# The second half of a layer's triangular solves moves from VectorE to GpSimd

## The chip, the cores and the metric

The kernel runs on one core of a Trainium2 chip. Its time is the device time of one execution in microseconds. A profiled execution also leaves a trace: when each instruction ran on TensorE (PE, with its weight loads PEld), VectorE (DVE), ScalarE (ACT) and GpSimd (POOL), and when SyncE (SP) issued DMAs.

## The reference

A two-layer network on 1040 tokens (16 learned ones ahead of 1024), width 1024. Layer 0 mixes with an attention and a state-space part, layer 1 with a gated delta rule of eight heads of width 128; an MLP follows each. Only layer 1's mixer matters here. With chunks of the sequence it computes, for each head, keys, queries and values (a product with a weight, a convolution over four tokens, silu), and then

```
lower = where(strict, beta * (k k^T) * decay, 0)
sol   = triangular_solve(I + lower, [v*beta, k*beta*exp(gcum)])
...                     # a scan over the chunks carries a 128x128 state
o     = rms_norm(o) * silu(z);  out = o @ w_out
```

## The kernel before

Products in float32 accuracy are made of three TensorE passes: weights and activations are split in a high part and a remainder, and high x high, high x low and low x high are summed in PSUM (L176, L177, L178). A weight tile comes by a DMA into one of two `wraw` buffers (L156), VectorE casts the high part (L165), and GpSimd subtracts for the remainder `wlo` (L166); four buffers of each hold weights ahead of their use.

Layer 1's mixer first makes the keys of the eight heads, then the queries, then per head the values and a gate. `conv_in` multiplies one tile of 128 features in three pieces of up to 352 tokens, each in one of three PSUM banks, and VectorE copies each piece out (L1343, tile `cx`). `conv_silu` scales on ScalarE (L1353), adds three shifted copies on VectorE (L1359, three instructions of 1040 elements) and applies silu on ScalarE (L1360, tile `cy`). `queries` then transposes on TensorE (L1469), reduces squares (L1471, L1472, norms `rq`), multiplies keys and queries (L1482, taken out by L1484), and multiplies by the decays on GpSimd in place (L1490).

The inverse of a 128 x 128 unit triangular matrix per head and chunk is made of blocks: four diagonal blocks of 32 x 32 are inverted alone, and `combine` joins them by products on TensorE (L1562 to L1587). The diagonal blocks of four heads, eight chunks and four blocks are 128, one for each partition. `solve_heads(half)` loads them (L1512, tile `sN`), `solve` inverts them (tile `sU`), and the result is stored (L1516), copied transposed on GpSimd (L1518) and stored again (L1520). Half 0 is heads 0 to 3, half 1 heads 4 to 7. `solve` takes 31 steps, each a product and a sum of an outer product's size:

```
v.tensor_tensor(p3, U3[:, 0:j, m]..., N3[:, m, m + 1:]..., op=ALU.mult)   # L1504
v.tensor_add(U3[:, 0:j, m + 1:], U3[:, 0:j, m + 1:], p3)                  # L1505
```

with j = m+1 and 31-m columns, so (m+1)(31-m) elements a partition: 31 in the first step, 256 in the middle, 31 in the last. Every instruction needs the one before it. A third, small solve (`solve_first`, tiles `U0` and `N0`, 16 x 16 on eight partitions) does the same for the sixteen leading tokens. Which engine runs a solve is a bit of the constant `SVE`:

```
yield from self.solve(128, 32, N, U, nc.gpsimd if SVE >> half & 1 else v)        # L1514
yield from self.solve(8, 16, N0, U0, nc.gpsimd if SVE >> 2 & 1 else nc.vector)   # L1530
```

The code writes instructions in one sequence, in which strands (keys and queries of even and odd heads, solves, combines, later chains, values and gates) take turns between the products. A scheduler of the framework then sorts them into one fixed order for each engine; semaphores make an engine wait where it needs another's result, and then all that stands behind waits too. The solve of half 1 can start when the keys of head 7 are done.

Of the kernel before, what the change touches and what calls it, by code (L numbers as in the profile page):

```python
# [1938 lines left out]
J3 = 2.5  # L1939
J4 = 5.0  # L1940
J5 = 4.0
CT, SVE, CJ = 0, 0, 0


PERIOD = 2
# [44 lines left out]
CT = 0  # L1990
# [53 lines left out]
CT = 0  # L2044
# [110 lines left out]
```

## Time and profile before

| | us |
|---|---|
| median of 3 runs (2943.26 to 2947.31) | 2943.39 |
| profiled execution | 2941.94 |
| its span, first to last instruction | 2940.1 |
| TensorE busy (94% of the span) | 2767.3 |
| VectorE busy (59%) | 1745.5 |
| GpSimd busy (44%) | 1307.8 |
| ScalarE busy (36%) | 1063.0 |

The second solve stands on VectorE from about 1703 to 1780 us of the span. The times below count from the span's start. In a timeline row stand the start, the duration, engine, line, operation, output and inputs, shapes and, in brackets, how long the engine was idle before it and what ended that. A group row has count, busy us and mean ns. A waits row has total us, times and the longest.

### The profile page before, as it was taken

What the parts mean: (1) busy time and instruction counts of PE and PEld (TensorE: products, weight loads), DVE (VectorE), ACT (ScalarE), POOL (GpSimd) and SP (SyncE); (2) the same over time, 40 slices, a digit from 0 to 9 for tenths busy, and PEclk for the clock granted to TensorE, in tenths of its full rate; (3) what the DMA queues carried; (4) which work ended last, traced back from release to release, by engine and by line L of the source; (5) the groups of instructions that cost most, each with busy time, mean ns of one, the idle gap of its engine ahead of it and who ended that gap; (6) DMA issues with size and microseconds to landing.
All of it is one profiled execution on the core that took longest, in us unless ns stands there. A gap on an engine that the chain in (4) does not pass through costs nothing. (4 is left out here: it accounts for less than half of the span.)

```text
span 2940.1 us, 44176 instructions
## 1 busy us (share of the span) xinstructions
PE 2767.3 (94%) x16488; PEld 2504.2 (85%) x16488; DVE 1745.5 (59%) x3107; ACT 1063.0 (36%) x2112; POOL 1307.8 (44%) x946
## 2 busy tenths in 40 slices
PE   7899999899999999999897978999998999999998
PEld 7689667788999999999887977899898888888887
DVE  8642768666755565555746896545538544444445
ACT  4111656554533332111436422433435433331101
POOL 5552325325577766432632123111125777664423
PEclk9889667889999999999998988999999999999999
DMA  3435312124333344221437667444334333442222
GB/s 129 158 121 157 80 57 80 49 87 166 129 116 115 100 142 152 90 85 44 140 88 221 195 201 235 127 132 149 109 117 153 107 109 111 136 165 93 95 82 89
DMA packets 209766, 360.99 MB, mean 123 GB/s; under 512 B 45488, under 2 KB 131200, under 8 KB 209552
## 3 DMA queue, kind: packets, MB, share of 16 engines
q1 hardware_dynamic: 205664, 353.49, 37.3%
q10 hardware_dynamic: 3888, 4.69, 0.4%
q8 instruction: 130, 2.13, 0.3%
q14 instruction: 84, 0.69, 0.1%
HBM read 247.07 MB, written 111.03 MB: 122 GB/s over the span
## 5 line engine op out<-in xcount | busy, mean ns | idle before, releaser
L166 POOL TENSOR_TENSOR wlo<-wraw,whi 128x1024 fp32r<-128x1024 f32 x125 | 305.0, 2452 | 730.5 <-ACT whi L163 238.7
L176 PE MATMUL mm<-ahi,whi 128*128 128x344 f32 (+2 forms) x1200 | 416.5, 348 | 41.3 <-DVE cx L1343 28.1
L178 PE MATMUL mm<-ahi,wlo 128*128 128x344 f32 (+2 forms) x1200 | 398.6, 332 | 2.3 <-DVE wlo L166 2.3
L177 PE MATMUL mm<-hl,whi 128*128 128x352 f32 (+4 forms) x1136 | 386.5, 340 | 0.0
L564 DVE TENSOR_TENSOR acc<-mm,acc 128x344 f32<-128x344 f32 (+4 forms) x308 | 177.3, 576 | 173.0 <-PE mm L178 173.0
L176 PEld LDWEIGHTS mm<-ahi,whi 128*128 128x128 f32 x1200 | 234.2, 195 | 50.2 <-DVE cx L1343 29.8
L178 PE MATMUL mm<-hh,wlo 128*128 128x352 f32 (+4 forms) x752 | 259.0, 344 | 2.5 <-POOL wlo L547 2.5
L176 PE MATMUL mm<-hh,whi 128*128 128x352 f32 (+4 forms) x752 | 259.2, 345 | 0.6 <-DVE acc L564 0.6
L178 PEld LDWEIGHTS mm<-ahi,wlo 128*128 128x128 f32 x1200 | 233.9, 195 | 4.3 <-DVE wlo L166 3.2
L564 DVE TENSOR_TENSOR acc<-tr,acc 128x344 f32<-128x344 f32 (+2 forms) x260 | 152.9, 588 | 139.7 <-PE tr L178 139.7
L177 PEld LDWEIGHTS mm<-hl,whi 128*128 128x128 f32 x1136 | 216.7, 191 | 11.1 <-issue 0.4
L178 PE MATMUL tr<-hh,wlo 128*128 128x512 f32 (+2 forms) x560 | 196.1, 350 | 0.0
L177 PE MATMUL tr<-hl,whi 128*128 128x512 f32 (+2 forms) x560 | 195.9, 350 | 0.0
L176 PE MATMUL tr<-hh,whi 128*128 128x512 f32 (+2 forms) x560 | 195.8, 350 | 0.0
L163 ACT CAST whi<-wraw 128x1024 fp32r<-128x1024 f32 x73 | 73.6, 1045 | 311.6 <-PE tr L177 287.2
L229 POOL TENSOR_TENSOR hl<-hr,hh 128x1040 fp32r<-128x1040 f32 (+1 forms) x56 | 135.6, 2431 | 76.4 <-ACT hh L228 53.7
L178 PEld LDWEIGHTS mm<-hh,wlo 128*128 128x128 f32 x752 | 142.1, 189 | 13.5 <-POOL wlo L547 3.1
L176 PEld LDWEIGHTS mm<-hh,whi 128*128 128x128 f32 x752 | 142.2, 189 | 10.9 <-DVE acc L564 0.9
L440 POOL TENSOR_TENSOR wlo<-sS,whi 128x512 fp32r<-128x512 f32 x104 | 144.4, 1391 | 13.6 <-ACT whi L439 13.4
L244 POOL TENSOR_TENSOR ssq<-ssq,sq 128x344 f32<-128x344 f32 (+2 forms) x84 | 90.9, 1082 | 84.5 <-ACT sq L243 76.4
L177 PE MATMUL mm<-hh,whi 128*128 128x344 f32 (+2 forms) x384 | 128.2, 334 | 0.0
L366 POOL TENSOR_TENSOR ssq_o<-ssq_o,sq 128x344 f32<-128x344 f32 (+4 forms) x84 | 93.9, 1118 | 76.4 <-ACT sq L365 75.9
(530 smaller groups left out, 7808.4 us busy)
## 6 DMA issues: line engine op xcount, KB each, us to landing
wraw<-w SPq DMA_DIRECT2D x128, 512.0 KB, 3.6
wraw<-wino SPq DMA_DIRECT2D x32, 512.0 KB, 5.2
hr<-hd SPq DMA_DIRECT2D x28, 520.0 KB, 5.5
hr<-hd SPq DMA_DIRECT2D x28, 512.0 KB, 4.3
dm<-dmd SPq DMA_DIRECT2D x16, 520.0 KB, 4.8
hsd<-hs SPq DMA_DIRECT2D x48, 172.0 KB, 1.9
hd<-u SPq DMA_DIRECT2D x52, 130.0 KB, 2.0
hd<-u SPq DMA_DIRECT2D x26, 256.0 KB, 2.8
```

What stands on the lines that cost most here:

```text
L163: nc.scalar.copy(hi[:, :n], raw[:, :n])
L166: (nc.vector if fast else nc.gpsimd).tensor_sub(lo[:, :n], raw[:, :n], f(hi[:, :n]))
L176: nc.tensor.matmul(pt, wh, h[:, o:o + n], start=i == 0, stop=False)
L177: nc.tensor.matmul(pt, wh, l[:, o:o + n], start=False, stop=False)
L178: nc.tensor.matmul(pt, wl, h[:, o:o + n], start=False, stop=i == len(kts) - 1)
L229: (lo_eng or nc.vector).tensor_sub(lo, src, f(hi))
L244: nc.gpsimd.tensor_add(st["ssq"][:, o:o + n], st["ssq"][:, o:o + n], sq[:, :n])
L366: nc.gpsimd.tensor_add(ssq[:, o:o + n], ssq[:, o:o + n], sq[:, :n])
L440: nc.gpsimd.tensor_sub(lo, src, f(hi))
L564: nc.vector.tensor_add(acc[m][:, o:o + n], pt, acc[m][:, o:o + n])
```

## The change

One constant: bit 1 of `SVE` is set, so that the solve of half 1 is issued to GpSimd. Its two memsets, 31 products and 31 sums move; the solve of half 0 and the small one stay on VectorE. No later line sets `SVE` again.

```diff
-CT, SVE, CJ = 0, 0, 0
+CT, SVE, CJ = 0, 2, 0
```

The scheduler sorts anew, so other instructions move too. Three places follow; numbers in names tell buffers apart.

VectorE, around the copy-out of the product of query head 5 (`cx_17147`; `mm_17149`, `mm_17179` and `mm_17212` are its three PSUM pieces), before:

```order
L1504 TENSOR_TENSOR sprod_17087<-sU_17079,sN_17078 128x220
L1505 TENSOR_TENSOR sU_17079<-sU_17079,sprod_17087 128x10x22
L1504 TENSOR_TENSOR sprod_17087<-sU_17079,sN_17078 128x231
L1343 TENSOR_TENSOR cx_17147<-mm_17149,rb_14159 128x352
L1343 TENSOR_TENSOR cx_17147<-mm_17179,rb_14159 128x344
L1343 TENSOR_TENSOR cx_17147<-mm_17212,rb_14159 128x344
L1359 SCALAR_TENSOR_TENSOR cy_17135<-cx_16543,gains_64,cy_17135 128x1040
L1505 TENSOR_TENSOR sU_17079<-sU_17079,sprod_17087 128x11x21
```

and after the change (`cy_17135` is query head 2, `U0` the small solve):

```order
L1359 SCALAR_TENSOR_TENSOR cy_17135<-cx_16543,gains_64,cy_17135 128x1040
L1504 TENSOR_TENSOR sprod_16937<-U0_16903,N0_16902 8x39
L1359 SCALAR_TENSOR_TENSOR cy_17135<-cx_16543,gains_64,cy_17135 128x1040
L1505 TENSOR_TENSOR U0_16903<-U0_16903,sprod_16937 8x13x3
L1359 SCALAR_TENSOR_TENSOR cy_17135<-cx_16543,gains_64,cy_17135 128x1040
L1504 TENSOR_TENSOR sprod_16937<-U0_16903,N0_16902 8x28
L1343 TENSOR_TENSOR cx_17147<-mm_17149,rb_14159 128x352
L1505 TENSOR_TENSOR U0_16903<-U0_16903,sprod_16937 8x14x2
L1343 TENSOR_TENSOR cx_17147<-mm_17179,rb_14159 128x344
```

The steps of half 1 are gone from VectorE; the copy-out now stands behind the three additions of head 2 and ahead of the end of the small solve.

GpSimd, behind the remainder `wlo_17264` of the weight for query head 7, before:

```order
L166 TENSOR_TENSOR wlo_17264<-wraw_17261,whi_17263 128x1024
L1490 TENSOR_TENSOR cy_16876<-cy_16876,eg_17083 128x1024
L1518 COPY sN_16186<-sU_16187 128x32x32
L166 TENSOR_TENSOR wlo_17440<-wraw_17437,whi_17439 128x1024
L166 TENSOR_TENSOR wlo_17739<-wraw_17736,whi_17738 128x1024
L1490 TENSOR_TENSOR cy_17034<-cy_17034,eg_17126 128x1024
```

After the change the solve's memsets and ten operations stand between the first and the second of these rows; in the middle of the solve stands:

```order
L1504 TENSOR_TENSOR sprod_17087<-sU_17079,sN_17078 128x252
L1505 TENSOR_TENSOR sU_17079<-sU_17079,sprod_17087 128x14x18
L1490 TENSOR_TENSOR cy_17034<-cy_17034,eg_17126 128x1024
L1518 COPY sN_16186<-sU_16187 128x32x32
L1339 MEMSET cx_17147 128x8
L1504 TENSOR_TENSOR sprod_17087<-sU_17079,sN_17078 128x255
```

Half 0's transposing copy (L1518) and query head 0's L1490 (`cy_17034`) now have 28 of the 62 operations ahead of them.

GpSimd, at the solve's end after the change:

```order
L1505 TENSOR_TENSOR sU_17079<-sU_17079,sprod_17087 128x27x5
L1504 TENSOR_TENSOR sprod_17087<-sU_17079,sN_17078 128x112
L1505 TENSOR_TENSOR sU_17079<-sU_17079,sprod_17087 128x28x4
L1504 TENSOR_TENSOR sprod_17087<-sU_17079,sN_17078 128x87
L166 TENSOR_TENSOR wlo_17440<-wraw_17437,whi_17439 128x1024
L1505 TENSOR_TENSOR sU_17079<-sU_17079,sprod_17087 128x29x3
```

The remainder `wlo_17440` of the weight for value head 0 stood ahead of query head 0's L1490 and now stands behind 57 operations of the solve; the next one, `wlo_17739`, comes later still.

## The prediction

> **What bounds the kernel now.** I read first the page's busy times, then the table by stretches around the solves, then TensorE's waits there, then the timelines of VectorE and GpSimd side by side.
>
> ```profile
> PE 2767.3 (94%) x16488; PEld 2504.2 (85%) x16488; DVE 1745.5 (59%) x3107; ACT 1063.0 (36%) x2112; POOL 1307.8 (44%) x946
> 1630.00:1686.00 56.00, 55.12 (x370) 52.97 (x369) 55.27 (x142) 22.75 (x48) 8.37 (x7) 1.00 0.56 182
> 1686.00:1724.00 38.00, 20.12 (x127) 19.48 (x127) 37.32 (x95) 5.68 (x7) 17.19 (x10) 0.77 0.56 198
> 1724.00:1741.00 17.00, 17.00 (x112) 16.84 (x113) 15.97 (x30) 4.43 (x6) 0.00 (x0) 0.91 0.61 187
> 1741.00:1784.00 43.00, 37.02 (x256) 35.83 (x255) 42.26 (x73) 11.35 (x14) 16.15 (x9) 0.93 0.71 246
> 1784.00:1816.00 32.00, 24.64 (x183) 22.65 (x182) 25.23 (x39) 7.83 (x11) 12.91 (x6) 0.93 0.61 193
> ```
>
> The first row is the whole span: TensorE is the bound. The others give, per stretch, its length and the busy time of PE, PEld, DVE, ACT and POOL, then the granted clock. From 1686 to 1784 us VectorE is busy 95.6 of 98 us and TensorE idles 23.9 us. Only what TensorE idles there can be won.
>
> ```profile
> 1699.05 1.12 PE L1469 MATMUL tr<-cst,cy 128*128 128x128 f32 x4 [4.83 <-ACT cy L1360]
> 1723.77 0.66 PE L176 MATMUL mm<-ahi,whi 128*128 128x352 f32 x1 [13.05 <-DVE cx L1343]
> 1763.86 0.63 PE L1469 MATMUL tr<-cst,cy 128*128 128x128 f32 x4 [2.13 <-DVE rq L1474]
> 1781.33 0.50 PE L176 MATMUL mm<-ahi,whi 128*128 128x352 f32 x1 [3.85 <-DVE cx L1343]
> ```
>
> Four stalls, 23.9 us, all behind VectorE (the first through ScalarE's silu, which waits for the last L1359). The largest is a product that wants a PSUM bank whose copy-out, L1343 of query head 5, stands on VectorE behind 21 operations of the second solve.
>
> **What leaves VectorE.** The second solve is two memsets and 62 products and sums.
>
> ```profile
> L1504 DVE TENSOR_TENSOR sprod<-sU,sN x31: 200/398/2342, 1704.5 to 1778.1; 128x31 f32<-128x31 f32 x2, 128x60 f32<-128x60 f32 x2, 128x87 f32<-128x87 f32 x2, 128x112 f32<-128x112 f32 x2
> L1505 DVE TENSOR_TENSOR sU<-sU,sprod x31: 172/373/2479, 1707.0 to 1779.4; 128x31 f32<-128x31 f32 x2, 128x60 f32<-128x60 f32 x2, 128x87 f32<-128x87 f32 x2, 128x112 f32<-128x112 f32 x2
> 1704.40:1780.00 75.60, 35.65 (x63) 2.36 (x2) 0.89 0.66 221
> 1703.25:1723.20 19.95, 15.15 (x24) 2.05 (x1) 0.75 0.60 214
> ```
>
> At the medians (398 and 373 ns) they would take 31 x 0.771 = 23.9 us; they took 35.65 us (third row, the operations on sU alone). The rest is waiting, and the next rows show for what. The last row says that 15.1 us of it, memset included, stand between 1703 us and the L1343 that TensorE waits for.
>
> **What that waiting is.** Rows of VectorE and GpSimd in the same microseconds:
>
> ```profile
> 1711.37 5.39 POOL L166 TENSOR_TENSOR wlo<-wraw,whi 128x1024 fp32r<-128x1024 f32 x2 [4.87 <-DVE whi L165]
> 1716.73 2.39 POOL L1490 TENSOR_TENSOR cy<-cy,eg 128x1024 f32<-128x1024 f32 x1
> 1712.24 2.32 DVE L1504 TENSOR_TENSOR sprod<-sU,sN 128x135 f32<-128x135 f32 x1
> 1714.60 2.32 DVE L1505 TENSOR_TENSOR sU<-sU,sprod 128x135 f32<-128x135 f32 x1
> 1716.95 2.34 DVE L1504 TENSOR_TENSOR sprod<-sU,sN 128x156 f32<-128x156 f32 x1
> 1719.33 0.32 DVE L1505 TENSOR_TENSOR sU<-sU,sprod 128x156 f32<-128x156 f32 x1
> 1723.20 1.36 DVE L1343 TENSOR_TENSOR cx<-mm,rb 128x352 f32<-128x352 f32 x3
> 1806.34 7.92 DVE L1359 SCALAR_TENSOR_TENSOR cy<-cx,gains,cy 128x1040 f32<-128x1040 f32 x3 [4.39 <-ACT cy L1353]
> 1806.56 6.59 POOL L1490 TENSOR_TENSOR cy<-cy,eg 128x1024 f32<-128x1024 f32 x2 [11.53 <-DMA eg<-gexp]
> 1649.88 1.12 DVE L1445 SCALAR_TENSOR_TENSOR nm<-tr,nb,dm 128x128 f32<-128x128 f32 x4
> 1650.10 2.39 POOL L166 TENSOR_TENSOR wlo<-wraw,whi 128x1024 fp32r<-128x1024 f32 x1 [12.90 <-PE tr L1442]
> ```
>
> A 0.3 us step with both inputs in SBUF lasts 2.32 us when GpSimd runs a 2.4 us subtraction, three times running: one of GpSimd, one of VectorE, one of GpSimd. At 1806 us three L1359 (1.28 us each alone) and two L1490 (2.4 us) interleave in the same way and take 7.92 us. L1445, which reads PSUM, runs four times in 1.12 us, undisturbed by the L166 that starts at 1650.10. So two-input SBUF work of the two engines takes turns, and GpSimd's solve will take turns with VectorE's.
>
> The Trainium skill (SBUF — State Buffer, section on the two separate sides) has the port pair shared by the two as an exclusive lock for a whole instruction; these rows agree (2.32 us for a 0.3 us step). Its page Perfetto Trace Analysis (section Optimizing Scalar/DVE Operations) adds that moving work between these two may therefore not help, which speaks against this change.
>
> **What GpSimd pays.** Its own small products and sums elsewhere:
>
> ```profile
> L686 POOL TENSOR_TENSOR s5bb<-s5bc,s5cr 128x256 f32<-128x256 f32 x1 | 0.6, 624 | 6.4 <-DVE s5t L674 6.4
> L743 POOL TENSOR_TENSOR s5mo<-s5bb,s5pi 128x512 f32<-128x512 f32 x4 | 4.5, 1114 | 0.0
> L547 POOL TENSOR_TENSOR wlo<-wraw,whi 128x256 fp32r<-128x256 f32 x4 | 2.9, 731 | 34.3 <-ACT whi L546 34.3
> L547 POOL TENSOR_TENSOR wlo<-wraw,whi 128x768 fp32r<-128x768 f32 x4 | 7.3, 1834 | 0.0
> ```
>
> A product costs 0.13 us and 1.91 ns an element (624 to 1114 ns over 256), a sum or difference 0.18 us and 2.15 ns (731 to 1834 ns over 512). Step m has (m+1)(31-m) elements, in all 5456, once as product and once as sum: 31 x 0.31 + 5456 x 4.06 ns = 31.8 us with GpSimd to itself. An operation of 31 to 256 elements takes 0.19 to 0.73 us. Shorter inner rows than any row shows could make it dearer (a bound above: twice); below, nothing suggests less than VectorE's 24 us.
>
> The Trainium skill (GPSIMD Engine Reference, section Elementwise — side-by-side cycle accounting) has about 2.6 cycles an element at 1.2 GHz, 2.17 ns; its slope agrees with the sums' 2.15. Without a fixed cost the solve would be 23.7 us by it, each operation some 0.13 us shorter, and by that estimate the sum below 5 us smaller.
>
> **The sum.**
>
> ```profile
> 1686.32 2.38 POOL L166 TENSOR_TENSOR wlo<-wraw,whi 128x1024 fp32r<-128x1024 f32 x1 [11.02 <-DVE whi L165]
> 1696.61 1.28 DVE L1359 SCALAR_TENSOR_TENSOR cy<-cx,gains,cy 128x1040 f32<-128x1040 f32 x1
> 1697.92 1.07 ACT L1360 ACTIVATE cy<-cy 128x1040 f32<-128x1040 f32 x1 [9.28 <-DVE cy L1359]
> L1484 DVE TENSOR_TENSOR dm<-tr,dm 128x512 f32<-128x512 f32 x4 | 2.7, 676 | 0.0
> L1472 DVE TENSOR_REDUCE rq<-csq 128x4 f32<-128x512 f32 x3 | 2.0, 667 | 0.0
> 1734.81 0.60 PE L1469 MATMUL tr<-cst,cy 128*128 128x128 f32 x4
> 1738.08 1.89 PE L1562 MATMUL tr<-T,nm 128*128 128x64 f32 x16
> 1721.86 2.36 SPq L1552 DMA_DIRECT2D U<-ublk  x4
> ```
>
> The two group rows are of VectorE from 1697.8 to 1723.2 us. GpSimd's order starts the solve behind the L166 that ends at 1688.7 us (first row), so at about 1689.5, while VectorE still has the first solve's tail, the eight-partition solve and L1359 to do. Just there VectorE has no slack, and its relief only begins at 1703.
>
> (a) To the last L1359 of query head 0, for which the 4.83 us stall waits: VectorE has 14 two-input steps left, so 13 solve operations and one L1490 (which stood there before too) come between. The operations on 31 to 135 elements (ten) 3.3 us, on 156 (two) and 175 (one) 1.4 us, 0.4 us of gaps; less 1.2 us in which VectorE does an L1343 and a reduction: +4 us on that stall.
>
> (b) From there to L1343 of query head 5 VectorE took 1697.8 to 1723.2 = 25.4 us. Without the second solve (15.0 us) and two L165 (1.2 us) that now come later, and with three L1359 (3.7 us) that now come before, 12.9 us are left. With them go 34 two-input steps. Between these GpSimd has 15 operations on 175 to 252 elements (9.2 us), then stops at an L1490 that overwrites what TensorE's L1482 reads, then that L1490 (2.4), L1518 (2.05, in GpSimd's column of the row from 1703.25) and ten operations on 247 to 256 (6.7), with gaps 21.3 us; 4.7 us of it lie beside VectorE's L1484 and L1472 (the two group rows). 12.9 + 16.6 = 29.5 us: +4 us more. The 13 us stall is thus not removed: its first cause goes, and GpSimd's turns take its place. TensorE starts head 6's product at about 1732 instead of 1723.8.
>
> (c) The silu of query head 3 stands behind six more such turns (4.0 us) and 8.8 us of VectorE's own (four L1343 1.9, three L1359 3.7, two L1472 1.3, one L1484 0.7, the rest small); with 1.1 us of ScalarE 13.9 us. TensorE came to its L1469 11.0 us after the product's start (1734.8 against 1723.8) and starts 0.5 us after the first L1343: +2.4 us.
>
> (d) After that VectorE has none of the remaining 41 solve operations (21.6 us in the first row below) and does not hold TensorE up: the stalls of 2.13 and 3.85 us go, -6.0 us. If GpSimd's turns still went on there, up to 12 us of them would come back.
>
> ```profile
> 1723.20:1780.00 56.80, 21.62 (x42) 0.31 (x1) 0.94 0.68 224
> 1814.55 0.69 DVE L165 CAST whi<-wraw 128x1024 fp32r<-128x1024 f32 x1 [0.29 <-DMA wraw<-wino]
> 1815.38 2.35 POOL L166 TENSOR_TENSOR wlo<-wraw,whi 128x1024 fp32r<-128x1024 f32 x1 [2.22 <-DVE whi L165]
> ```
>
> (e) Queues. On GpSimd the first half's L1518 now waits behind 28 solve operations, from 1704 to about 1722 us, and on SP the loads for head 0's combine stand behind its store and behind the eight-partition result: about 1738 instead of 1721.9. They take 7 us to issue and 4 to land, 1749; TensorE reaches L1562 (1738.1 before, plus 8 and 2.4) at about the same time, so nothing is added, but no cover is left. The wlo for value head 0 stands on GpSimd behind 57 of the 62 solve operations, which end at about 1750 (1732, then 11 us of their own and some 6 of turns); TensorE wants it after the L1469 of 1763.86, about 8 us later than that now. The next ones are fetched, cast and subtracted much later in the order than before (0.69 + 2.35 us each, rows above, after their 512 KB load). Nothing hides them where a gate product starts: 0 to 5 us over the chains, I take 2.
>
> Sum: 4 + 4 + 2.4 - 6 + 2 = +6.4 us on the profiled run's 2941.9; the median of the runs lies 1.4 us higher, so 2950 us.
>
> **Rivals.** VectorE wins (faster): if its steps never wait for GpSimd's short ones, (a) to (c) are 0 except that L1343 comes at 1697.8 + 12.9 = 1710.7, just when TensorE stopped: the 13.05 us stall shrinks to 0.5, and -12.6 - 6 + 2 = -16.6, 2927 us. It decides once the turns cost less than about half of what I count. Against it: every row above where the two met. A draw: VectorE's many 0.2 us steps pass two at a time while GpSimd, whose every operation needs the one before, gets ready; the turns in (b) fall from 16.6 to some 10 us, (b) becomes 22.9 - 25.4 = -2.5, (c) 0: 4 - 2.5 - 6 + 2 = -2.5, 2941 us. Dear small rows (much slower): operations twice as long add about 5 in (a), 16 in (b), 4 in (c), in all 6.4 + 25 = +31, 2975 us, and the solve ends so late that wlo becomes the bound; only the unknown of the inner rows speaks for it. That the change does nothing is excluded by the order: all 64 instructions change engines.
>
> **How the numbers follow.** My forecast 0.40, VectorE wins 0.25, a draw 0.27, dear rows 0.08. A measurement tells no change from about 0.2%, 5.9 us. Faster 0.25, same 0.28, slower 0.47: my forecast is only just outside the band. Range: 2927 (VectorE wins) to 2966 (half way to dear rows); the forecast's own 2944 to 2957.
>
> **What would show it.** Right: VectorE's steps on eight partitions and L1359 at 0.4 us or more above their old times between 1690 and 1735; GpSimd's operations near 0.19 to 0.73 us but spaced wider; TensorE's stalls from 1690 up to query head 6's product at 26 us in all (4.83 + 13.05 = 17.9 now), however they are spread, and none behind VectorE from there to the value product's end. Wrong: a product for head 6 that starts before 1715 (VectorE wins), a GpSimd solve that lasts past 1765 (dear rows), or new waits on L166 among the chains above 5 us.

## The result: 2966.8 us, slower by 0.8%

| | before | after |
|---|---|---|
| median (6 runs each, same chip) | 2943.32 us | 2966.8 us |
| lowest to highest | 2942.84 to 2947.31 | 2958.23 to 2978.59 |
| profiled execution | 2941.94 | 2965.1 |
| its span | 2940.1 | 2963.3 |

The ratio is 1.0079, 95% interval 1.0065 to 1.0093. The sign is as forecast, but 23.5 us were lost instead of 6.7, just outside the range.

First TensorE's waits between 1690 and 1940 us, after the change (in all, times, the longest):

```profile
PE tr L1562 <- DMA T<-tblk: 19.8, 1, 19.8
PE mm L176 <- DVE cx L1343: 7.1, 2, 6.3
PE tr L1469 <- ACT cy L1360: 6.4, 3, 3.1
PE tr L1646 <- DVE S L1662: 3.3, 2, 2.1
PE tr L1602 <- ACT cy L1360: 3.0, 1, 3.0
```

Before, the first row did not exist, and the stall on L1343 alone was 13.05 us. The stalls behind VectorE became smaller, and one stall on a DMA is now the largest. Where it comes from stands in the timelines of TensorE, SP and GpSimd after the change (start, duration, idle time before and what ended it):

```profile
1717.68 0.66 PE L176 MATMUL mm<-ahi,whi 128*128 128x352 f32 x1 [6.29 <-DVE cx L1343]
1753.34 3.65 PE L1562 MATMUL tr<-T,nm 128*128 128x64 f32 x16 [19.81 <-DMA T<-tblk]
...
1719.12 0.32 SPq L1520 DMA_DIRECT2D tblk<-sN  x1
...
1726.89 0.33 SPq L1536 DMA_DIRECT2D u<-u0d  x1
1748.93 1.81 SPq L1552 DMA_DIRECT2D U<-ublk  x4
1750.79 0.94 SPq L1554 DMA_DIRECT2D T<-tblk  x2
...
1745.81 0.27 POOL L1505 TENSOR_TENSOR sU<-sU,sprod 128x31 f32<-128x31 f32 x1
1746.14 1.92 POOL L1518 COPY sN<-sU 128x1024 f32<-128x1024 f32 x1
1747.91 1.00 POOL L1545 MEMSET U<- 128x1024 f32 x1
```

Between 1727 and 1749 us SP issues nothing. The longest of its waits from 1690 to 1765 us names the reason:

```profile
SPq L1552 <- POOL U L1545: 21.7, 1, 21.7
```

TensorE came to head 0's combine (L1562) at 1733.5 us and waited for its tile T. The blocks had been stored since L1520 of 1719 us. SP didn't load them, because the first load, into U, waits for the memset of U (L1545), and that memset stands on GpSimd behind the last step of the second solve and the copy L1518. Before, it ran at this place:

```profile
1719.13 0.95 POOL L1545 MEMSET U<- 128x1024 f32 x1
```

A second loss lies further back. Here are the stretches from the last copy-out of value head 1 to that of value head 3, before and after (length; busy time of PE, PEld, DVE, ACT, POOL; granted clock):

```profile
1816.14:1922.52 106.38, 104.72 (x757) 92.67 (x756) 44.07 (x111) 38.32 (x88) 16.09 (x16) 0.97 0.54 170
```

```profile
1829.92:1943.74 113.82, 107.04 (x739) 94.88 (x738) 53.78 (x114) 37.27 (x84) 24.96 (x17) 0.93 0.56 176
```

The same stretch takes 7.4 us longer: TensorE idles 5.1 us more and is busy 2.3 us more, at a lower clock. VectorE and GpSimd are each busy 9 to 10 us more. On VectorE that is three more casts of weights (L165), which the kernel before had made earlier and two of which take 4.58 and 1.97 us instead of 0.69, and slower L1359 (1.83 instead of 1.30 us each on average).

Set against the start of this region (the profiled run after was 1.0 us ahead at 1690 us, and already at 1467 us), the difference of the two profiles runs like this: -5.1 us when TensorE starts query head 6's product, -3.5 us when it reaches L1562, +16.3 us when it starts it, +14.8 us at value head 1, +22.2 us at value head 3, +24.2 us at the end.

### The profile page after: what moved, and what is told of

The parts are those of the page before. It is cut to its first block, busy times and chain, and to the rows that moved or that the text cites. A ratio compares the mean times of both kernels' runs of the same rounds, so it can differ in the third digit from the quotient of the medians.

```text
span 2963.3 us, 44157 instructions
## 1 busy us (share of the span) xinstructions
PE 2775.3 (94%) x16488; PEld 2509.3 (85%) x16488; DVE 1731.3 (58%) x3043; ACT 1063.6 (36%) x2112; POOL 1351.7 (46%) x1010
## 3 DMA queue, kind: packets, MB, share of 16 engines
q8 instruction: 130, 2.13, 0.3%
## 5 line engine op out<-in xcount | busy, mean ns | idle before, releaser
L166 POOL TENSOR_TENSOR wlo<-wraw,whi 128x1024 fp32r<-128x1024 f32 x125 | 306.9, 2467 | 721.2 <-DVE whi L165 260.7
L177 PEld LDWEIGHTS mm<-hl,whi 128*128 128x128 f32 x1136 | 217.1, 191 | 10.9 <-issue 0.2
L440 POOL TENSOR_TENSOR wlo<-sS,whi 128x512 fp32r<-128x512 f32 x104 | 144.2, 1389 | 14.8 <-ACT whi L439 14.7
```

The lines of the kernel that those rows point to most:

```text
L166: (nc.vector if fast else nc.gpsimd).tensor_sub(lo[:, :n], raw[:, :n], f(hi[:, :n]))
L177: nc.tensor.matmul(pt, wh, l[:, o:o + n], start=False, stop=False)
L440: nc.gpsimd.tensor_sub(lo, src, f(hi))
```

## The experiments

**Theories.** A: GpSimd works in order, and the combine's memsets L1545 and L1546 stand behind the solve; SP's loads behind them, and TensorE behind these. B: the loss is the engines' turns and late weights, and would come up at the next wait if this one went. Later two more were needed: C, that any short instruction on GpSimd behind the solve is late, one after the other; and D against E, on the second loss. Each edit lets the scheduler sort anew, so where it mattered a control has the same edit with both solves on VectorE. Ratios are to the kernel before, run on the same chip; its medians there were 2943.8 to 2945.5 us. Profiled executions differ before any edit acts (the same copy-out stands at 1460.7 to 1474.9 us in the eighteen of them), so times are medians, and the profiles, one for each version, serve for places.

### The combine's memsets on VectorE

```diff
-        nc.gpsimd.memset(U[:, :1024], 0.0)
-        nc.gpsimd.memset(T[:, :1024], 0.0)
+        z = nc.vector if h == 0 else nc.gpsimd
+        z.memset(U[:, :1024], 0.0)
+        z.memset(T[:, :1024], 0.0)
```

(Lines behind it have numbers one higher in these kernels: L1579 is L1578 of the kernel before.)

> The changed kernel, with one edit: the two memsets of the combine for head 0 (L1545, L1546) run on VectorE instead of GpSimd, where they stand behind the whole second solve. Theory A (SP's loads for that combine wait for GpSimd's memset, and TensorE's L1562 waits for them, 19.8 us): the wait at L1562 falls to 0 to 6 us, SP's 21.7 us wait for that memset goes, and the time falls by 14 to 20 us against the changed kernel's 2966.8, to 2947 to 2953 us. Theory B (the loss is the turns of the two engines and late weights; the 19.8 us would otherwise be lost at the next wait): the wait at L1562 goes, but another of similar size stands right behind it, and the time stays at 2958 us or more.

Measured: 2958.2 us, ratio 1.0047 (1.0031 to 1.0063). The wait at L1562 and SP's 21.7 us went. But TensorE now stalled 9.95 us at the combine's third product. The rows of TensorE, VectorE, ScalarE and GpSimd:

```profile
1763.36 0.66 PE L1579 MATMUL tr<-T,nm 64*64 64x64 f32 x4 [9.95 <-issue]
...
1763.06 0.29 DVE L1574 STREAM_TRANSPOSE T<-U 32x32 f32<-32x32 f32 x2
...
1758.75 1.16 ACT L1353 ACTIVATE cy<-cx,gains 128x1040 f32<-128x1040 f32 x1 [13.55 <-POOL cx L1339]
1759.82 0.34 ACT L1571 COPY U<-tr 32x256 f32<-32x256 f32 x1
...
1754.26 0.27 POOL L1505 TENSOR_TENSOR sU<-sU,sprod 128x31 f32<-128x31 f32 x1
1754.59 1.91 POOL L1518 COPY sN<-sU 128x1024 f32<-128x1024 f32 x1
1756.38 2.34 POOL L1490 TENSOR_TENSOR cy<-cy,eg 128x1024 f32<-128x1024 f32 x1
1758.66 0.10 POOL L1339 MEMSET cx<- 128x8 f32 x1
```

ScalarE stood at the first step of the next silu (L1353), which waits for a 0.1 us pad memset (L1339); that stands on GpSimd behind the solve's last step, L1518 and L1490, and L1353 starts when it is done. ScalarE's copy for the combine (L1571) waited behind L1353, and VectorE's transposes into T (L1574) behind that. The profile names no releaser for TensorE's stall, but it ends when the second of these transposes does. So A named the first wait rightly and had the time wrong; B's time (2958 us or more) just held, and another wait followed as it said, though for GpSimd's order and not for turns or weights. 8.6 us of 20 were kept.

> The kernel before, with both solves on VectorE, and the same edit of the two memsets (L1545, L1546 of head 0 on VectorE). It is the control: in the kernel before these memsets stood ahead of everything that waits. Both theories: no wait at L1562, and 2943 us, give or take 4 (two memsets of under 1 us more on VectorE at its busiest place).

Measured: 2949.7 us, 1.0017 (1.0005 to 1.003), no wait at L1562; some 5 us worse than before, a little outside. Why is open: with the pad memsets on VectorE as well, the control below is back at the time of the kernel before, so that two memsets on a full VectorE are no sufficient reason.

### The second solve later

```diff
-                yield from self.wait_for(("k", 4 * half + 3))
+                yield from self.wait_for(("k", 4 * half + 3), *([("U", 0)] if half else []))
```

> The changed kernel, but the second solve (still on GpSimd) starts only when head 0's combine is done. Theory A: GpSimd's queue is free when the combine's memsets come, no wait at L1562, and what was gained ahead of it (6.1 us) is kept or grows, since VectorE meets no turns there: 2935 to 2945 us. Theory B: the turns only move to later places, and weights come late there: 2955 us or more.

Measured: 2957.6 us, 1.0056 (1.0042 to 1.0069): A's number failed, and B's (2955 us or more) held. No wait for the combine's loads was left, and TensorE started head 6's product at 1715.7 us. But then:

```profile
1813.23 1.12 PE L1469 MATMUL tr<-cst,cy 128*128 128x128 f32 x4 [37.72 <-ACT cy L1360]
...
1811.05 1.16 ACT L1353 ACTIVATE cy<-cx,gains 128x1040 f32<-128x1040 f32 x1 [39.99 <-DMA qTd<-cy]
...
1805.32 2.34 POOL L1490 TENSOR_TENSOR cy<-cy,eg 128x1024 f32<-128x1024 f32 x1
```

A silu waits for a buffer, the buffer for a store of a query tile, the store for the product L1490, and L1490 stands on GpSimd behind 54 solve steps. The block moved, and met the next short instruction; turns and late weights, B's reason, are not what TensorE waited for.

> The kernel before, both solves on VectorE, but the second one starts only when head 0's combine is done. It prices VectorE's backlog without any work of GpSimd's. If what TensorE idles behind VectorE between 1690 and 1784 us (23.9 us) comes from the place of the second solve in VectorE's order, the 13 us stall goes and the time is 2926 to 2934 us; if the same operations cost as much at the later place, it stays at 2940 us or more.

Measured: 2943.7 us, 0.9998 (0.9986 to 1.001). The 13 us stall did go (3.98 us were left of it), but stalls of 6.8 and 3.4 us came up at 1770 and 1783 us, where the same steps now stood. As the second half of the expectation says, the backlog is of operations, not of their place.

### What the solve can be worth at all

> The kernel before, without 60 of the 62 products and sums of the second solve (only the first product and sum are left): the result of heads 4 to 7 is not computed rightly, and nothing takes VectorE's place. It prices the most that any move of this solve off VectorE could win. If VectorE's backlog between 1690 and 1784 us is what TensorE idles for there, 13 to 17 us go and the time is 2926 to 2932 us; if the idle time has other causes or comes back later, it is 2938 us or more.

Measured: 2938.1 us, 0.9981 (0.9965 to 0.9998). Leaving the work out wins about 7 us (0.6 to 10 by the interval), less than half of the 16.6 that I had counted for a VectorE without it. TensorE still stalls 8.53 us for L1343 of query head 5. VectorE's and GpSimd's rows ahead of that copy-out, in this run:

```profile
1709.62 2.31 DVE L1506 TENSOR_TENSOR U<-U,sprod 8x28 f32<-8x28 f32 x1
1711.96 2.25 DVE L1505 TENSOR_TENSOR sprod<-U,N 8x15 f32<-8x15 f32 x1
1714.25 2.28 DVE L1506 TENSOR_TENSOR U<-U,sprod 8x15 f32<-8x15 f32 x1
1716.45 1.35 DVE L1343 TENSOR_TENSOR cx<-mm,rb 128x352 f32<-128x352 f32 x3
...
1709.14 5.05 POOL L166 TENSOR_TENSOR wlo<-wraw,whi 128x1024 fp32r<-128x1024 f32 x2 [2.40 <-DVE sprod L1505]
1714.15 2.34 POOL L1490 TENSOR_TENSOR cy<-cy,eg 128x1024 f32<-128x1024 f32 x1
```

Three steps of the small solve, 0.2 us each, take turns with three long instructions of GpSimd: 6.8 us. In the kernel before, three steps of the second solve stood there and paid the same. It is the length of GpSimd's instruction that sets what a turn costs, and in both kernels there was some step to pay it.

> The kernel before, but with only the small solve (eight partitions, 32 instructions) on GpSimd. It puts a much shorter block into GpSimd's queue (my estimate from the changed kernel's rows: 30 operations of 0.2 to 0.35 us, 8 to 10 us) at the same place. Theory C (everything on GpSimd behind the block is late by what the block takes): no wait of TensorE for the combine's loads above 5 us, since head 0's combine needs its memsets only at 1735 us; VectorE loses 6 us of work ahead of the copy-out that TensorE waits for 13 us, so that this stall shrinks by 2 to 6 us: 2938 to 2944 us. Theory B (any work of GpSimd's there costs VectorE its turns): the stall does not shrink, 2944 to 2950 us.

The edit: `SVE` is 4. Measured: 2948.0 us, 1.001 (0.9996 to 1.0025), in B's range. No wait for the combine's loads, as C says, but the stall was 13.66 us and did not shrink. Again two steps pay 2.55 and 2.44 us just ahead of L1343, beside an L1490 and an L166. That is not B's reason either: GpSimd's own small solve was over at 1706 us by then.

### Pad memsets too, then three decay products

```diff
-            nc.gpsimd.memset(xs[t][:, 0:8], 0.0)
+            (nc.vector if len(tiles) == 1 else nc.gpsimd).memset(xs[t][:, 0:8], 0.0)
```

> The changed kernel with two edits: the two memsets of head 0's combine and the small memsets that clear the first eight columns of each query tile (L1339, 0.1 us each) run on VectorE instead of GpSimd. Theory C (GpSimd's queue runs in order, and everything short that stands on it behind the solve is late: first the combine's memsets, and once those are moved, L1339, for which ScalarE's first step of the next silu waited 13.55 us): the 9.95 us stall at the combine's third product goes too, and the time falls by another 8 to 12 us against the run with the combine's memsets alone (2958.2), to 2946 to 2950 us. Theory B (turns and late weights cost it): 2955 us or more, with the stall back at another place.

Measured: 2951.5 us, 1.0019 (1.0008 to 1.003): 6.7 us better than with the combine's memsets alone, a little less than C's. The stall at the third product stayed at 8.68 us, with a new releaser. ScalarE, SP and GpSimd:

```profile
1744.14 1.16 ACT L1353 ACTIVATE cy<-cx,gains 128x1040 f32<-128x1040 f32 x1 [10.91 <-POOL cy L1490]
...
1744.13 0.32 SPq L1365 DMA_DIRECT2D qTd<-cy  x1
...
1739.53 0.27 POOL L1505 TENSOR_TENSOR sU<-sU,sprod 128x31 f32<-128x31 f32 x1
1739.87 2.02 POOL L1518 COPY sN<-sU 128x1024 f32<-128x1024 f32 x1
1741.77 2.34 POOL L1490 TENSOR_TENSOR cy<-cy,eg 128x1024 f32<-128x1024 f32 x1
```

Solve, copy, L1490, store, silu: the third thing behind the solve.

> The kernel before, both solves on VectorE, with the same two edits of memsets. The control: the earlier control (combine's memsets alone) was at 2949.7, against 2944.1 before. Both theories: 2944 to 2952 us.

Measured: 2944.5 us, 0.9993 (0.9984 to 1.0002). So with these edits the change costs 7 us, against a control with the same edits, instead of 23.5.

> The second solve on GpSimd only after head 0's combine, and the two kinds of memsets on VectorE. With the later start alone TensorE came 14 us earlier to 1770 us and then waited 37.7 us for a silu behind L1339. Theory C: that stall goes and most of the 14 us stay: 2928 to 2936 us. Rival: the next thing on GpSimd behind the solve (the products L1490, whose stores SP waits for) takes the place of L1339: 2942 us or more.

Measured: 2956.1 us, 1.0041 (1.0026 to 1.0057). C's number failed and its rival held: a 33.2 us stall behind L1490, for which SP's store waited 25.5 us.

```diff
-        nc.gpsimd.tensor_mul(qT[:, 16:NT], ...)
+        (v if h in (2, 3, 4) else nc.gpsimd).tensor_mul(qT[:, 16:NT], ...)
```

> The changed kernel with both kinds of memsets on VectorE, and beside that the decay products (L1490) of query heads 2, 3 and 4, which stood on GpSimd just behind the solve, on VectorE. Theory C (the 8.7 us stall that was left at the combine's third product is GpSimd's queue once more: a store waits for L1490, ScalarE's next silu waits for the store's buffer): that stall falls below 3 us, and the time falls from 2951.5 by 2 to 6 us (three products of 1.2 us more on VectorE go against it), to 2945 to 2949 us. Otherwise the stall stays at 6 us or more, and the time at 2951 or above.

Measured (on top of both kinds of memsets): 2943.7 us, 1.0004 (0.999 to 1.0019). That is 7.8 us, a little more than C's 2 to 6. No stall at the combine is left, and the time is that of the kernel before. Three kinds of short instructions moved from behind the solve took the 23 us back in three steps: 2966.8, 2958.2, 2951.5, 2943.7. The last step has no control with both solves on VectorE, so it isn't shown how much of it the moved products would win there too.

### The second loss: casts

This edit puts the casts of the weights (L165) on ScalarE, for all tiles of the projection:

```diff
-            self.w_conv[self.order[i]] = self.weight(self.io["wino"][self.order[i]])
+            self.w_conv[self.order[i]] = self.weight(self.io["wino"][self.order[i]], act=True)
```

> The changed kernel with both kinds of memsets on VectorE, and beside that the casts of the projection's weights (L165) on ScalarE instead of VectorE. In the run without the last edit (2951.5, its control 2944.5) a second loss of 11 us stands among the first chains, after all solves: TensorE has stalls of 1.6 to 2.6 us there that the kernel before doesn't have, and its granted clock is 0.89 instead of 0.95. Theory D: weights come there without lead and in bunches, and a cast on VectorE that takes turns with GpSimd's subtractions and memsets (4.58 us instead of 0.69 in the changed kernel) holds up the chain steps behind it. Then casts on ScalarE take 4 to 8 us of the 11 away, against the same edit with both solves on VectorE. Theory E: the second loss comes with whatever runs ahead, and isn't of these casts: the difference to the same edit with both solves on VectorE stays at 7 us or more.

> The kernel before, both solves on VectorE, with both kinds of memsets on VectorE and the casts of the projection's weights (L165) on ScalarE: the control of the run beside it. 22 casts of 0.7 us leave VectorE, of which three stand between 1686 and 1724 us, where TensorE waits for it: 2 us fewer there, 2940 to 2946 us, if ScalarE's own steps are not held up; up to 2952 if they are.

Measured: 2949.2 us, 1.0011 (0.9996 to 1.0027), and the control 2951.4 us, 1.0024 (1.001 to 1.0037). The difference of the two is -2 us, against +7 without the edit, as D says. The control, though, lost 7 us by the edit itself, more than expected, and the version with the change won only 2; why is open. In the profiles the stretch from value head 1 to value head 3 is 109.1 us against 108.6 in the control; with casts on VectorE it was 117.5 against 106.6. So by the profiles the casts on VectorE were the second loss; the times alone don't price it. What one of them met, after the change, on VectorE, GpSimd and TensorE (L1646 to L1662 are steps of the chain, the scan that carries the 128x128 state):

```profile
1866.22 4.58 DVE L165 CAST whi<-wraw 128x1024 fp32r<-128x1024 f32 x1
1870.73 0.33 DVE L1662 SCALAR_TENSOR_TENSOR S<-S,dgegl,tr 128x128 f32<-128x128 f32 x1
...
1866.05 2.38 POOL L166 TENSOR_TENSOR wlo<-wraw,whi 128x1024 fp32r<-128x1024 f32 x1 [5.32 <-DVE whi L165]
1868.38 0.95 POOL L1545 MEMSET U<- 128x1024 f32 x1
1869.26 0.95 POOL L1546 MEMSET T<- 128x1024 f32 x1
...
1871.11 0.49 PE L1646 MATMUL tr<-S,ch 128*128 128x128 f32 x2 [2.12 <-DVE S L1662]
```

A cast of 0.69 us ended only when three instructions of GpSimd had, and the chain's step L1662 stood behind it.

The last pair casts on ScalarE for the values' and gates' weights alone (`act=self.order[i] >= 16`), on the version with the decay products moved:

> The changed kernel with both kinds of memsets and three decay products on VectorE (2943.7 us), and beside that the casts (L165) of the weights of values and gates alone on ScalarE; those of the queries stay on VectorE. Theory D (the second loss of 10 us among the first chains is of these casts, which take turns with GpSimd's subtractions ahead of a chain's steps): TensorE's stalls of 2.5 and 2.0 us between 1840 and 1890 us go, and with them the lower clock behind them, and the time is 2934 to 2940 us. Theory E (it comes with whatever runs ahead): 2942 us or more.

> The kernel before, both solves on VectorE, with both kinds of memsets on VectorE (2944.5 us), and the casts of the weights of values and gates on ScalarE. The control: it has no second loss that could go, 2942 to 2948 us.

Measured: 2939.4 us, 0.9987 (0.9973 to 1.0002), in D's range. Its stalls of 2.5 and 2.0 us became 0.81 and 1.62, and the stretch went from 116.8 to 111.5 us. The control measured 2950.4 us, 1.0021 (1.0007 to 1.0035), above what was expected. That is 11 us between the two (the control lacks the moved decay products), but against the kernel before the 4 us aren't told apart from nothing. None of the versions beats it clearly, and without the solve at all it is 7 us.

### The other half

> The first half's solve on GpSimd, the second half's and the small one on VectorE. Between 1630 and 1686 us GpSimd is busy 8.4 of 56 us and VectorE 55.3. Theory C (it is a matter of what stands behind the solve): the solve ends at about 1670 us, only pad memsets and a weight's remainder are behind it, VectorE comes to 1690 us without backlog, and of the 23.9 us of stalls up to 1784 us some 8 to 15 go: 2930 to 2940 us. Rival (a solve on GpSimd costs the turns wherever it is, and what VectorE gains is given back later, as when the second solve was left out and only 7 us were won): 2940 us or more.

> As the run beside it, with the memsets of the query tiles' first columns and of head 0's combine on VectorE, so that nothing short stands behind the first solve on GpSimd. If the pad memsets behind the solve cost anything there, this run is faster by 2 us or more than the one beside it; if TensorE has cover enough, the two agree within 2 us.

The edit: `SVE` is 1. Measured: 2950.7 us, 1.0024 (1.0009 to 1.0039), and with the memsets on VectorE 2948.2 us, 1.0015 (1.0002 to 1.0029); the two agree within their scatter. C's number failed here: a place where GpSimd has nothing to do did not make it pay. TensorE stalls 7.0 us at 1680 us, on ScalarE, which waits for GpSimd's solve; the row of ScalarE's waits there:

```profile
ACT csq L1421 <- POOL sU L1505: 13.0, 1, 13.0
```

A square on ScalarE waits 13 us for the last step of the solve. What ties the two is open. In the kernel's code `csq`, which the square writes, and `sprod`, which that step reads, come from the same ring of ten scratch buffers (`tmp`), so the square may have waited for the solve to let go of one; but in the kernel before the same square did not wait, though that solve lasted to 1704 us there, and no run gave `sprod` a buffer of its own. With the memsets on VectorE the stall was 7.0 us again, so that it isn't one of theirs. The solve there ended at 1679.3 us, not 1670: it had started at 1633, as before, and took 46 us.

## Why the prediction was wrong

**(a) and (b), the turns ahead of query head 6's product: wrong in sign.** Forecast were +4 and +4 us and 26 us of stalls; there were 10.9 us, and the product started at 1717.68 us, 6.1 us earlier, 1.0 of which the run was ahead anyway. The first L1469 stalled 3.08 us instead of 4.83. From the last L1359 to L1343 VectorE took 21.9 us; I had 29.5, and the draw 22.9. Ahead of the last L1359 the turn with an L1490 was gone: GpSimd came to that product only at 1696.73 us. GpSimd's steps were sized rightly (0.25 to 0.74 us where no long instruction of VectorE came between, the solve over at 1746 us against "about 1750"). What failed is one turn of GpSimd for each of VectorE's steps (VectorE after the change):

```profile
1693.90 1.28 DVE L1359 SCALAR_TENSOR_TENSOR cy<-cx,gains,cy 128x1040 f32<-128x1040 f32 x1
...
1702.34 0.23 DVE L1504 TENSOR_TENSOR sprod<-sU,sN 128x87 f32<-128x87 f32 x1
1702.50 0.60 DVE L1504 TENSOR_TENSOR sprod<-U,N 8x64 f32<-8x64 f32 x1
1703.04 0.23 DVE L1505 TENSOR_TENSOR sU<-sU,sprod 128x87 f32<-128x87 f32 x1
1703.19 0.56 DVE L1505 TENSOR_TENSOR U<-U,sprod 8x64 f32<-8x64 f32 x1
...
1717.12 0.51 DVE L1343 TENSOR_TENSOR cx<-mm,rb 128x352 f32<-128x352 f32 x1
```

Two steps pass for each of GpSimd's, one at its old time and one some 0.35 us longer. That is the mechanism of the rival "a draw", to which I gave 0.27. If VectorE's own work there was the 12.9 us of the sum, the turns came to some 9.0 us instead of 16.6, and 4.3 of these are two long ones beside an L1490 (steps of 2.37 and 2.32 us). The three 2.3 us turns with L166 and L1490 of the kernel before are not the error: they were in the 15.0 us that the sum took off. The Trainium skill (SBUF — State Buffer, section on the two separate sides) has the lock last for a whole instruction; that agrees: 2.3 us is the length of an L166 or L1490, and 0.35 us the rest of a 0.6 us step. The conclusion that I drew from it, that the lock speaks against the change, did not follow: short instructions make a cheap lock.

**(c), the silu of query head 3: near in size, by luck.** From head 6's product to L1562 TensorE took 15.9 us instead of 14.3, +1.5 us against +2.4. But it hardly waited for the silu, whose row on TensorE names no stall:

```profile
1730.21 0.66 PE L1469 MATMUL tr<-cst,cy 128*128 128x128 f32 x4
```

TensorE was busy 15.73 of the 15.85 us, at a granted clock of 0.85 instead of 0.89. The turns that were to delay the silu are not there: the last three L1359 ahead of it took 1.29 us each.

**(d), the stalls that go: in part.** The two of 2.13 and 3.85 us became one of 2.53 and two below 1 (0.78 and 0.81); another, 6.79 us at L1602, which I had not counted, became 3.00. On the path from L1562's start to value head 1 that is -1.5 us against -6: TensorE idled 6.1 us less there, as much as forecast by chance, but it was busy 4.7 us longer, L1562 alone 3.65 us instead of 1.89.

**(e), the queues: this is the step that failed.** I wrote that "nothing is added, but no cover is left" at L1562, with loads issued at about 1738 and landed at 1749. They were issued from 1748.93 on. I had followed L1518 and SP's stores past the solve, but not the two memsets L1545 and L1546, which the kernel before had at 1719.13 us and the change behind the last step; of five kinds of instructions that others wait for behind the solve (L1518, L166, L1545 with L1546, L1339, L1490) I had followed the first two. TensorE was also there 15 us earlier than I had it (1733.5 against 1748.5), so that the missing cover cost 19.8 us. Moved away, these instructions were worth 15 us with the memsets (2966.8 to 2951.5) and 23 with L1490 (2943.7, without a control), as much as the change had lost. The weights' lateness, the other term of (e), was taken at +2 (0 to 5) and came out at 7.4 us in the profile; its mechanism, weights without lead, was right, but I priced only TensorE's direct wait for them (it was 1.4 us), not what the bunched casts do to the chains.

By place, the profile after differs from the sum like this: +16.3 us instead of +10.4 where TensorE starts the combine, then -1.5 instead of -6 up to value head 1, +7.4 instead of +2 up to value head 3, and +2.0 behind it, where I had nothing.

So the direction came out right by luck, for a reason that the sum did not hold. In the profile of the run with all three kinds moved, the path is 4.8 us ahead of the kernel before at value head 1 (both set to 1690 us) and 5.6 us behind at value head 3: a gain up to the chains, given back by the casts. "Dear small rows" is out by the rows of GpSimd. "VectorE wins" is out too: even without the solve the stall was 8.53 us, not 0.5.

## What to carry to other kernels

Before a long chain goes to an engine that runs in order, list everything else that is issued to this engine in the same stretch, down to the 0.1 us memsets, and for each who waits for it; here the chain's own steps were sized rightly, and what waited behind them cost some 23 us. Where two engines take turns, take the price of a turn from the length of the partner's instruction: many short ones are cheap, a 2.4 us one beside 0.2 us steps is dear. And bound a move by a run with the work left out: here the bound was about 7 us, where 23.9 us of stalls were in view.

## What the runs showed of the hardware

**A stall costs more than its length.** TensorE's granted clock behind a stall, after the change (the 2.12 us stall ends at 1871.1) and in the kernel before (1.49 us, ends at 1905.1):

```profile
1871.10:1873.00 1.90, 1.89 (x11) 1.21 (x11) 0.35 (x1) 0.37 (x1) 1.90 (x1) 0.92 0.41 65
1873.00:1879.00 6.00, 6.00 (x23) 5.51 (x23) 2.30 (x7) 2.47 (x5) 0.25 (x1) 0.50 0.72 232
```

```profile
1907.00:1913.00 6.00, 6.00 (x52) 5.49 (x50) 2.67 (x5) 0.60 (x2) 0.00 (x0) 1.00 0.00 0
```

After 2.12 us of idling TensorE ran for 6 us at half its clock, which costs some 3 us on top of the stall. Over the region from 1690 to 2080 us of all these runs, every stall longer than 2.0 us was followed by 8 us at 0.50 to 0.84, be it 2.1 or 37 us long; of those between 1.0 and 1.6 us more than half were followed by 1.00. The sum of the prediction counted stalls at their length. The Trainium skill (TensorE: Matmul & The Clock Gate, section on HAM oscillation) warns of idle gaps above some 3.4 us; here 2.0 to 2.6 us already did it.

**Turns aren't strict.** Where the prediction had one for one, the cast of 4.58 us lost three in a row, and half of VectorE's steps beside the solve lost none.
